# A hybrid attention and pooling block: pooling's splits and maps between the steps of the last k and q tiles, first loads issued there

## The chip, the cores and the metric

The kernel runs on one core of one Trainium2 chip. The metric is the device time of one execution in microseconds (us). Each core has five engines with queues of their own: TensorE (PE in the profile, its weight loads PEld), VectorE (DVE), ScalarE (ACT), GpSimd (POOL, here Pool) and SyncE (SP), which in this kernel only issues DMA transfers. Each engine works its queue strictly in order and waits on semaphores that the other engines and the transfers raise. Matmuls write into eight PSUM banks of 128 x 512 float32; a bank is used again when its reader has let it go.

## What is computed

One layer of a streaming encoder over 16 meta tokens and 1024 frames, 1024 wide. Cut to what matters here:

```python
n1 = _rmsnorm(h, norm1_w)
q, k, v, fg, u = jnp.split(n1 @ w_in, ...)
q, k = per-head rmsnorm of q and k
a_out = _forgetting_attention(q, k, v, cumsum(log_sigmoid(fg + b)))
pooled[g] = trailing mean of u[g] over 2, 4, 8, 16 frames - u[g]
p_out = einsum("blgc,gcd->blgd", pooled, w_pool) * pool_scale
h = h + concat(a_out, p_out) @ w_out
h = h + (silu(n2 @ w_gate) * (n2 @ w_up)) @ w_down
```

Every matrix product is done in three matmuls, on a high and a low part of each operand (high x high, high x low, low x high). So each operand is *split* first: ScalarE copies it into the high part (`A.activation(..., AF.Copy)`), and VectorE or Pool subtracts that from the original to give the low part.

## The kernel before

All tiles are transposed: features on the partitions, 1040 positions along the free axis. The program is one list in which the order for every engine is written by hand; closures that are put off go to the list `later`, and each call of `run_later` lets the next step of every pending tile run.

The input projection goes tile by tile in `order`: q0, k1, q1, k2, q2, then the four pooling groups u3 to u0, then k3 and q3. A k tile has three column chunks (348, 346, 346), a q tile two of 512, and each chunk takes 24 matmuls (`proj_mm`, tile `pj`, L446 to L448). `qk_evac` (from L306) does the head norm of a chunk in steps: ScalarE squares the bank twice (`sqh`, `sq`) and VectorE subtracts (`sql`, L312); one turn of `later` on, two matmuls sum over the head (`ss`, L316 and L317), VectorE adds, ScalarE takes logarithm and exponential, Pool multiplies (L322); a turn later VectorE does three more and so frees the bank (L325 to L327); then ScalarE's high part (L330), then VectorE's low part (L333) and, behind a tile's last chunk, the store of both parts to DRAM (L336).

Pooling: Pool adds shifted copies of u (L459), VectorE finishes (L464). In the last q tile, which runs its two chunks in step over eight k blocks of the input (L485 to L487), the four groups are split (L490, in the helper at L132), then the pool weights (L495); behind the tile `pool_map` maps each group with 2 x 3 matmuls (tile `pm`, L526 to L528), ScalarE and VectorE evict and split the result (`mph` L529, `mpl` L530).

Output projection: a job is one of eight row blocks and one half of the frames, 12 matmuls of 512 columns for the pooled half of the mix (tile `o`, L544 to L546). Its weights come by `out_load` (tile `wos`, L558), are split by ScalarE (L573) and Pool (L574), and VectorE adds the bank to a row of h, loaded by `h_load` (L565, add L603). The jobs wait in `fill_q`; `fill(1)` puts one into the program, and they serve as work for TensorE between the steps of attention.

Attention: `stack(h)` loads a head's q and k (L632 to L634), `vload(h)` its values (L639). A unit (h, b) is a head and one half of the frames. For each unit `mx_steps` computes scores (tile `s`, L666 to L669) whose maxima VectorE takes (`mp`, L670), and `mt` transposes the negated maxima (L689), after which the unit's steps run: logits (`st`), two exponentials on ScalarE, the low part `pl` on Pool or VectorE (L735), products with v (`pv`). Before the first unit come its scores and some output jobs; `RAMP` says how many times a job and two scores of the second unit are put ahead of the loop, and `FILL[n]` how much of a job goes into each step of unit n.

SP's queue takes its transfers in program order; a store that waits for its data holds those behind it.

Of the kernel before, what the change touches and what calls it, by code (L numbers as in the profile page):

```python
# [7 lines left out]
FT = mybir.dt.float32  # L8
FR = mybir.dt.float32r
AF = mybir.ActivationFunctionType  # L10
OP = mybir.AluOpType
# [3 lines left out]
KT = D // 128  # L15
META = 16
SEQ = 1024
L = META + SEQ
# [5 lines left out]
ST = 9  # L24
# [15 lines left out]
MID = 1  # L40
VST = 3
AGE = 2
RAMP = 2
FILL = [12 / 40] * 8 + [16 / 40] * 8


@with_exitstack
def block_kernel(ctx, tc, hT, n1w, w_f, w_v, w_u, w_qk, b_f, qnw, knw, w_pool, pscale, w_out, n2w, w_g, w_up, w_d, outT):
# [12 lines left out]
    def ut(cols, dt=FT, s="u"):  # L61
        return U.tile([128, cols], dt, tag="u", bufs=NU, padded_shape=None, name=nm(s))
# [4 lines left out]
    def ps(s="ps"):  # L67
        return PSP.tile([128, 512], FT, tag="ps", name=nm(s))
# [57 lines left out]
    def split_w(stage, cols, mk, he, le):  # L126
        h, l = mk(cols, FR, "wh"), mk(cols, FR, "wl")
        if he is A:
            A.activation(h, stage, AF.Copy)
        else:  # L130
            he.tensor_copy(h, stage)
        le.tensor_tensor(l, stage, f(h), op=OP.subtract)  # L132
        return h, l
# [6 lines left out]
    def aux(cols, dt=FT, s="ax"):  # L140
        return U.tile([128, cols], dt, tag="aux", bufs=NAUX, name=nm(s))
# [117 lines left out]
    def v_evac(j, p):  # L259
        sz = min(128, L - 128 * j)  # L260
        for i in range(2):
            if len(vst) < 2 * VST:
                t = ut(768, FR, "vst").rearrange("p (h c) -> p h c", c=192)
                V.tensor_copy(t[:, :, 64:128], onesf[:, None, 0:64].to_broadcast([128, 4, 64]))
                vst.append(t)
            t, src = vst[2 * (j % VST) + i], p[:sz, 256 * i:256 * i + 256].rearrange("p (h c) -> p h c", c=64)
            A.activation(t[:sz, :, 0:64], src, AF.Copy, scale=rcol[:sz, j:j + 1])
            V.scalar_tensor_tensor(t[:sz, :, 128:192], src, rcol[:sz, j:j + 1], f(t)[:sz, :, 0:64], op0=OP.mult, op1=OP.subtract)
            nc.sync.dma_start(vsd[j, :sz, 768 * i:768 * i + 768], f(t)[:sz].rearrange("p h c -> p (h c)"))
# [32 lines left out]
    def qk_tile(c, i):  # L302
        n = L if c == "k" else SEQ
        return c, i, n, ut(n, FT, c + "32"), ut(n, FR, c + "h"), ut(n, FR, c + "l")

    def qk_evac(p, n, cols, w, tile, C):  # L306
        name, i, width, t32, th, tl = tile
        out = t32[:, C]
        h, l, s = hs(n, FR, "sqh"), hs(n, FR, "sql"), hs(n, FT, "sq")
        A.activation(h, p[:, :n], AF.Square)  # L310
        A.activation(s, p[:, :n], AF.Square)
        V.tensor_tensor(l, s, f(h), op=OP.subtract)  # L312

        def rest():
            p2 = ps("ss")
            mm(p2[:, :n], bones, h, start=True, stop=False)  # L316
            mm(p2[:, :n], bones, l, start=False, stop=True)  # L317
            t, g, s2 = hs(n, FT, "t"), hs(n, FT, "g"), hs(n, FT, "s2")
            V.scalar_tensor_tensor(t, qrow[:, cols], 64.0 * EPS, p2[:, :n], op0=OP.mult, op1=OP.add)
            A.activation(g, t, AF.Ln)  # L320
            A.activation(g, g, AF.Exp, scale=-0.5)  # L321
            G.tensor_tensor(s2, t, g, op=OP.mult)  # L322

            def last():
                V.scalar_tensor_tensor(s2, s2, -0.5, g, op0=OP.mult, op1=OP.mult)  # L325
# [12 lines left out]
                later.append(high)  # L338
            later.append(last)
        later.append(rest)  # L340

    def run_later(now):
        for g in now:
            g()
# [8 lines left out]
    vp = vn  # L353
# [61 lines left out]
    def load_w(x):  # L415
        c, i = order[x]
        return load((w_u[i] if c == "u" else w_qk[2 * i + (c == "k")]).rearrange("p k f -> p (k f)"), 1024, aux)
# [23 lines left out]
    def proj_mm(w, o, n):  # L441
        wh, wl = w
        p = ps("pj")
        for k in range(KT):
            W = slice(128 * k, 128 * k + 128)
            mm(p[:, :n], wh[:, W], xh[k][:, o:o + n], start=k == 0, stop=False)  # L446
            mm(p[:, :n], wl[:, W], xh[k][:, o:o + n], start=False, stop=False)  # L447
            mm(p[:, :n], wh[:, W], xl[k][:, o:o + n], start=False, stop=k == KT - 1)  # L448
        return p
# [14 lines left out]
            V.scalar_tensor_tensor(pooled[g], src[:, META:], 1.0 / (2 << g), pooled[g], op0=OP.mult, op1=OP.subtract)  # L464
        late_u.append(last)

    v_evac(ST - 1, vp)
    for x, (c, i) in enumerate(order):
        if x + 2 < len(order):
            staged.append(load_w(x + 2))  # L470
        if c == "u":
            t = ut(L, FT, "u")
        else:
            t = qk_tile(c, i)
        if x + 1 == len(order):

            now, later[:] = later[:], []
            run_later(now)
            wps = aux(512, FT, "wps")
            nc.sync.dma_start(wps, w_pool.rearrange("p g f -> p (g f)"))  # L480
            pb = [ps("pj") for _ in CHQ]
            for k in range(KT):
                W = slice(128 * k, 128 * k + 128)
                for p, (o, n) in zip(pb, CHQ):
                    mm(p[:, :n], wcur[0][:, W], xh[k][:, o:o + n], start=k == 0, stop=False)  # L485
                    mm(p[:, :n], wcur[1][:, W], xh[k][:, o:o + n], start=False, stop=False)
                    mm(p[:, :n], wcur[0][:, W], xl[k][:, o:o + n], start=False, stop=k == KT - 1)  # L487
                if k % 2:
                    g = 3 - k // 2
                    psplit[g] = split_w(pooled[g], SEQ, ut, A, V)  # L490
                if k == 2:
                    now, later[:] = later[:], []
                    run_later(now)
                if k == 4:
                    wph, wpl = split_w(wps, 512, aux, A, V)  # L495
            for p, (o, n) in zip(pb, CHQ):
                qk_evac(p, n, slice(o, o + n), qw, t, slice(o - META, o - META + n))
            break
        for o, n in CHQ if c == "q" else CH3:
            p = proj_mm(wcur, o, n)  # L500
            if o < 512 and n + o < 600 and x + 1 < len(order):
                wnext = split_w(staged.pop(0), 1024, ut, A, V)
            now, later[:] = later[:], []
            if o > 512 and late_u:
                late_u.pop(0)()
            if c == "u":
                V.tensor_tensor(t[:, o:o + n], p[:, :n], rb[:, o:o + n], op=OP.mult)
            else:
                a = o - META if c == "q" else o
                qk_evac(p, n, slice(o, o + n), kw if c == "k" else qw, t, slice(a, a + n))  # L510
            run_later(now)
        if c == "u":
            pool(i, t)
        wcur = wnext


    mixp = [None] * 4

# [95 lines left out]

    vhb = [[ut(192 * nj, FR, "vh").rearrange("p (j c) -> p j c", c=192) for nj in (5, 4)] for _ in range(2)]
    Mc = [const([128, 4, 68], FR, f"Mc{i}") for i in range(2)]
    for t in Mc:
        G.memset(f(t), 0.0)  # L620
# [13 lines left out]
        dma(f(K2)[64:68], f(KAT[0])[4 * h:4 * h + 4])  # L634

    def vload(h):
        for t, j, n, sz in ((0, 0, 5, 128), (1, 5, 3, 128), (1, 8, 1, 16)):
            o = j - 5 * t
            nc.sync.dma_start(f(vhb[h % 2][t])[:sz, o:o + n], vsd[j:j + n, :sz, 192 * h:192 * h + 192].rearrange("j p c -> p j c"))  # L639
# [148 lines left out]

    units = [(h, b) for h in range(NH) for b in range(2)]
    out_fill(0, lambda: mixp, ((4, 8),), range(0, 8), True)  # L790
    wo0 = out_load(0)
    out_fill(4, lambda: mixa[0:2], ((0, 2),), range(0, 8), False)
    wo[0] = out_split(wo0)
    h_load(0)
    wo[1] = out_load(1)
    stack(0)
    vload(0)
    for g in (3, 2, 1, 0):
        pool_map(g)
        now, later[:] = later[:], []  # L800
        run_later(now)
    s0 = mx_steps(*units[0])
    for x, s in enumerate(s0):
        s()
        if x % 2:
            fill(1)
            now, later[:] = later[:], []
            run_later(now)
    while later:
        now, later[:] = later[:], []  # L810
        run_later(now)
    stack(1)
    fin = mt(*units[0])
    fill(1)
    fin()
# [635 lines left out]
```

## Time and profile before

| | us |
|---|---|
| median of 3 runs | 1159.59 (1158.83 to 1160.97) |
| the profiled execution | 1161.34 |
| its span, first to last instruction | 1159.6 |
| TensorE busy | 1127.5 |
| VectorE, ScalarE, Pool busy | 747.6, 478.1, 373.9 |
| mean granted TensorE clock | 0.938 of full speed |

The span is what the profile's times are counted in, from its first instruction. Busy time says what an engine worked, not what it held up; for that there are the list of waits, the timeline of each engine and the windows, which give busy time and granted clock for a stretch. The last k tile begins at about 197 us, attention at about 254, the second half of the layer at about 488.

### The profile page before, as it was taken

The numbers are of one execution on the slowest core, as the hardware profiler recorded it, in microseconds if no ns is written. First come the engines' busy times: TensorE is split into PE (matmuls) and PEld (weight loads), VectorE is DVE, ScalarE is ACT, GpSimd is POOL, SyncE is SP. The second block draws the span as 40 slices with busy tenths as digits, with TensorE's granted clock in tenths as the row PEclk, the third lists the DMA queues.
The fourth block names the chain that finished last, engine by engine and source line by source line (L and its number), as shares of the span: only waits on it lengthen the run. The fifth ranks groups of instructions, "written<-read, shape, count | busy, mean of one in ns | idle before, by whom it ended". The sixth has DMA issues, their size and how long they took to land.

```text
span 1159.6 us, 14738 instructions
## 1 busy us (share of the span) xinstructions
PE 1127.5 (97%) x5327; PEld 932.9 (80%) x5327; DVE 747.6 (64%) x1185; ACT 478.1 (41%) x868; POOL 373.9 (32%) x292
## 2 busy tenths in 40 slices
PE   7999999889999999888999999999999999999998
PEld 6778899778888888666788888888888888888886
DVE  7555873764556676799654554455545569778976
ACT  7344531624555666534332332233123335343532
POOL 0001244223434556538644345334533510000000
PEclk9889999988999999899899999999999999999999
DMA  7133340574544343230323132213221379543452
GB/s 240 75 131 144 125 145 33 138 220 101 138 107 99 93 98 114 100 118 0 109 73 95 52 109 73 96 50 110 73 82 64 132 256 373 187 158 100 153 193 109
DMA packets 62425, 141.10 MB, mean 122 GB/s; under 512 B 7616, under 2 KB 18496, under 8 KB 62352
## 3 DMA queue, kind: packets, MB, share of 16 engines
q1 hardware_dynamic: 52528, 123.86, 33.6%
q10 hardware_dynamic: 9824, 16.30, 3.8%
q8 instruction: 42, 0.69, 0.2%
q14 instruction: 31, 0.25, 0.1%
HBM read 105.17 MB, written 34.77 MB: 121 GB/s over the span
## 4 chain that ended last, share of the span: by engine, by line
PE 83%; DVE 8%; DMA 3%; ACT 2%; issue 2%; POOL 1%; SPq 0%; ACTq 0%; POOLq 0%; DVEq 0%
PE gu L1118 10%; PE gu L1117 10%; PE gu L1116 10%; PE d L1358 6%; PE d L1360 6%; PE d L1359 6%; PE pj L447 3%; PE pj L448 3%; PE pj L446 3%; PE o L544 2%; PE st L721 2%; PE o L545 2%; PE o L546 2%; PE v L254 2%; PE v L255 2%
## 5 line engine op out<-in xcount | busy, mean ns | idle before, releaser
L1117 PE MATMUL gu<-cb,ws 128*128 128x512 f32 x560 | 221.1, 395 | 4.2 <-DVE ws L1107 4.1
L1118 PE MATMUL gu<-cb,ws 128*128 128x512 f32 x560 | 221.0, 395 | 0.0
L1116 PE MATMUL gu<-cb,ws 128*128 128x512 f32 x560 | 221.0, 395 | 0.0
L1107 DVE TENSOR_TENSOR ws<-wst,ws 128x512 fp32r<-128x512 f32 x120 | 97.1, 809 | 124.9 <-ACT ws L1106 124.9
L1117 PEld LDWEIGHTS gu<-cb,ws 128*128 128x128 f32 x560 | 105.6, 189 | 29.8 <-DVE ws L1107 5.1
L1106 ACT ACTIVATE ws<-wst 128x512 fp32r<-128x512 f32 x120 | 69.9, 621 | 137.4 <-POOL wst L1101 129.7
L1118 PEld LDWEIGHTS gu<-cb,ws 128*128 128x128 f32 x560 | 105.7, 189 | 24.6
L1116 PEld LDWEIGHTS gu<-cb,ws 128*128 128x128 f32 x560 | 105.4, 188 | 24.3
L1358 PE MATMUL d<-hd,wd 128*128 128x512 f32 x308 | 121.4, 394 | 0.0
L1359 PE MATMUL d<-hd,wd 128*128 128x512 f32 x308 | 121.2, 394 | 0.0
L1360 PE MATMUL d<-hd,wd 128*128 128x512 f32 x308 | 121.2, 394 | 0.0
L735 POOL TENSOR_TENSOR pl<-p,ph 128x512 fp32r<-128x512 f32 (+4 forms) x66 | 72.6, 1112 | 56.9 <-ACT p L729 47.9
L1130 POOL TENSOR_TENSOR e<-e,e 128x512 f32<-128x512 f32 x20 | 29.6, 1479 | 158.2 <-DVE e L1143 105.4
L447 PE MATMUL pj<-xh,wl 128*128 128x346 f32 (+2 forms) x216 | 72.9, 337 | 0.0
L448 PE MATMUL pj<-xl,wh 128*128 128x346 f32 (+2 forms) x216 | 72.8, 337 | 0.0
L446 PE MATMUL pj<-xh,wh 128*128 128x346 f32 (+2 forms) x216 | 72.8, 337 | 0.0
L322 POOL TENSOR_TENSOR s<-t,g 128x346 f32<-128x346 f32 (+2 forms) x20 | 22.2, 1118 | 155.3 <-ACT g L321 144.6
L670 DVE TENSOR_REDUCE mp<-s 128x1 f32<-128x144 f32 (+6 forms) x112 | 52.5, 504 | 30.3 <-PE s L669 28.4
L728 ACT ACTIVATE ph<-st 128x512 fp32r<-128x512 f32 (+4 forms) x88 | 46.4, 528 | 58.4 <-PE st L721 55.2
L1360 PEld LDWEIGHTS d<-hd,wd 128*128 128x128 f32 x308 | 57.9, 188 | 13.5
L1359 PEld LDWEIGHTS d<-hd,wd 128*128 128x128 f32 x308 | 57.9, 188 | 13.3
L1358 PEld LDWEIGHTS d<-hd,wd 128*128 128x128 f32 x308 | 57.9, 188 | 13.4
(287 smaller groups left out, 2525.2 us busy)
## 6 DMA issues: line engine op xcount, KB each, us to landing
wst<-in_w_d SPq DMA_DIRECT2D x77, 256.0 KB, 3.4
wst<-in_w_g SPq DMA_DIRECT2D x22, 512.0 KB
wst<-in_w_up SPq DMA_DIRECT2D x22, 512.0 KB, 3.4
wst<-hidd SPq DMA_DIRECT2D x22, 512.0 KB, 7.7
K<-kd SPq DMA_DIRECT2D x24, 260.0 KB, 6.6
vsd<-vst SPq DMA_DIRECT2D x16, 384.0 KB, 2.4
Q<-qd SPq DMA_DIRECT2D x24, 256.0 KB, 7.8
wst<-in_w_d SPq DMA_DIRECT2D x11, 512.0 KB, 5.8
```

The lines of the kernel that those rows point to most:

```text
L446: mm(p[:, :n], wh[:, W], xh[k][:, o:o + n], start=k == 0, stop=False)
L447: mm(p[:, :n], wl[:, W], xh[k][:, o:o + n], start=False, stop=False)
L448: mm(p[:, :n], wh[:, W], xl[k][:, o:o + n], start=False, stop=k == KT - 1)
L735: sub.tensor_tensor(pl[:sz, o0:o1], p32[:sz, o0:o1], f(ph)[:sz, o0:o1], op=OP.subtract)
L1106: A.activation(t[:, :512], src, AF.Copy)
L1107: E.tensor_tensor(t[:, 512:], src, f(t)[:, :512], op=OP.subtract)
L1116: mm(p, w[:, W], c[:, :512], start=k == 0, stop=False)
L1117: mm(p, w[:, Wl], c[:, :512], start=False, stop=False)
L1118: mm(p, w[:, W], c[:, 512:], start=False, stop=k == 3)
L1358: mm(p, w[:, W], h[:, LO], start=i == 0, stop=False)
L1359: mm(p, w[:, Wl], h[:, LO], start=False, stop=False)
L1360: mm(p, w[:, W], h[:, HI], start=False, stop=i == NPR - 1)
```

## The change

It moves code; no instruction is added or left out on TensorE. Four parts:

- The pooled groups 3, 2 and 1 are split after the three chunks of the last k tile, the pool weights after the third; group 0 after the first of the eight steps of the last q tile. The four maps stand between its steps 2 to 6. The ss pair of k's third chunk stands behind the first step.
- `out_load` of the first two jobs, `h_load` of the first two rows and head 0's `stack` and `vload` are issued in the last k tile and the first two steps of q; the first weights are split after step 6.
- Behind the q tile, each of five output jobs is followed by a turn of `later` and (from the second on) one score step; `stack(1)` stands in the third of these.
- `RAMP` is 1, and `FILL` 11/37 for the first eight units, 17/40 for the others.

```diff
-RAMP = 2
-FILL = [12 / 40] * 8 + [16 / 40] * 8
+RAMP = 1
+FILL = [11 / 37] * 8 + [17 / 40] * 8
...
             run_later(now)
+            if x + 2 == len(order):
+                psplit[3 - a] = split_w(pooled[3 - a], SEQ, ut, A, V)
+                if a == 2:
+                    wo[0] = out_load(0)
+                    wph, wpl = split_w(wps, 512, aux, A, V)
...
+    for k in range(KT):
...
+        turn()
+        if k == 0:
+            psplit[0] = split_w(pooled[0], SEQ, ut, A, V)
+            h_load(0)
+            wo[1] = out_load(1)
+        if k == 1:
+            h_load(1)
+            stack(0)
+            vload(0)
+        if 2 <= k < 6:
+            pool_map(5 - k)
+        if k == 6:
+            wo[0] = out_split(wo[0])
...
-    for x, s in enumerate(s0):
-        s()
-        if x % 2:
-            fill(1)
-            now, later[:] = later[:], []
-            run_later(now)
-    while later:
-        now, later[:] = later[:], []
-        run_later(now)
-    stack(1)
+    for x in range(5):
+        fill(1)
+        turn()
+        if x:
+            s0.pop(0)()
+        if x == 2:
+            stack(1)
+    s0.pop(0)()
     fin = mt(*units[0])
     fill(1)
     fin()
```

Three places in the queues. First TensorE where the last k tile ends (`ss` of its third chunk, `pj` the banks of the q tile), before and now:

```order
L316 MATMUL ss_1940<-sqh_1918,bones 128x346
L317 MATMUL ss_1940<-sql_1919,bones 128x346
L485 MATMUL pj_1956<-xh_127,wh_1841 128x512
L486 MATMUL pj_1956<-xh_127,wl_1842 128x512
L487 MATMUL pj_1956<-xl_128,wh_1841 128x512
L485 MATMUL pj_1957<-xh_127,wh_1841 128x512
```

```order
L786 MATMUL pj_1966<-xh_127,wh_1849 128x512
L787 MATMUL pj_1966<-xh_127,wl_1850 128x512
L788 MATMUL pj_1966<-xl_128,wh_1849 128x512
L786 MATMUL pj_1967<-xh_127,wh_1849 128x512
L787 MATMUL pj_1967<-xh_127,wl_1850 128x512
L788 MATMUL pj_1967<-xl_128,wh_1849 128x512
L316 MATMUL ss_1974<-sqh_1934,bones 128x346
L317 MATMUL ss_1974<-sql_1935,bones 128x346
L786 MATMUL pj_1966<-xh_156,wh_1849 128x512
```

The pair ss went behind six matmuls of the q tile.

Second SP's queue behind the loads for head 0 (`kd`, `qd` the stores of the last tiles, `wos` output weights, `h` rows of h, `Q`, `K` head 1), before and now, each as far as the first loads of head 1:

```order
L336 DMA kd<-kl_1815 128x1040
L336 DMA qd<-qh_1938 128x1024
L336 DMA qd<-ql_1939 128x1024
L558 DMA wos_2182<-in_w_out 128x512
L565 DMA h_374_2184<-in_hT 128x1024
L632 DMA Q_381_2230<-qd 64x1024
L632 DMA K_383_2232<-kd 64x1040
```

```order
L336 DMA kd<-kh_1822 128x1040
L336 DMA kd<-kl_1823 128x1040
L509 DMA wos_2140<-in_w_out 128x512
L509 DMA wos_2204<-in_w_out 128x512
L516 DMA h_376_2206<-in_hT 128x1024
L583 DMA Q_380_2231<-qd 64x1024
L583 DMA K_382_2233<-kd 64x1040
```

The two stores of q went behind; now they stand after all eight transfers of `stack(1)`:

```order
L585 DMA K_383_2234<-kat_702 4x1040
L336 DMA qd<-qh_1964 128x1024
L336 DMA qd<-ql_1965 128x1024
L509 DMA wos_2267<-in_w_out 128x512
L516 DMA h_387_2269<-in_hT 128x1024
L509 DMA wos_2329<-in_w_out 128x512
L516 DMA h_396_2331<-in_hT 128x1024
```

Third VectorE ahead of the second unit's mt (`h` the adds of output jobs, `mp` the maxima of scores, `mx` and `Mc` the three small steps that mt waits for), before and now:

```order
L670 TENSOR_REDUCE mp_2295<-s_2327 128x1
L670 TENSOR_REDUCE mp_2295<-s_2331 128x1
L603 TENSOR_TENSOR h_387_2249<-o_2311,h_387_2249 128x512
L670 TENSOR_REDUCE mp_2295<-s_2367 128x1
L670 TENSOR_REDUCE mp_2295<-s_2371 128x1
L670 TENSOR_REDUCE mp_2295<-s_2402 128x1
L670 TENSOR_REDUCE mp_2295<-s_2406 128x1
L670 TENSOR_REDUCE mp_2295<-s_2410 128x1
L682 TENSOR_REDUCE mx_2415<-mp_2295 128x4
L683 TENSOR_SCALAR Mc_2048<-mx_2415 128x4
L684 SCALAR_TENSOR_TENSOR Mc_2048<-mx_2415,Mc_2048 128x4
```

```order
L554 TENSOR_TENSOR h_387_2269<-o_2333,h_387_2269 128x512
L623 TENSOR_REDUCE mp_2349<-s_2391 128x1
L623 TENSOR_REDUCE mp_2349<-s_2395 128x1
L623 TENSOR_REDUCE mp_2349<-s_2426 128x1
L623 TENSOR_REDUCE mp_2349<-s_2430 128x1
L623 TENSOR_REDUCE mp_2349<-s_2435 128x1
L623 TENSOR_REDUCE mp_2349<-s_2439 128x1
L623 TENSOR_REDUCE mp_2349<-s_2443 128x1
L635 TENSOR_REDUCE mx_2448<-mp_2349 128x4
L636 TENSOR_SCALAR Mc_830<-mx_2448 128x4
L637 SCALAR_TENSOR_TENSOR Mc_830<-mx_2448,Mc_830 128x4
```

The add in the middle moved two maxima up, and the row it adds to is that of the fourth job, not of the third. In the programs for TensorE, five score steps now stand between the second unit's logits ahead and its mt, where there were three; unit (3, 1) has no output job in place of two, and seven stand ahead of the loop in place of five.

## Rows read from the trace of the kernel before

**Rows 1.** the page's busy times: engine, us, share of the span, instructions.

```profile
PE 1127.5 (97%) x5327; PEld 932.9 (80%) x5327; DVE 747.6 (64%) x1185; ACT 478.1 (41%) x868; POOL 373.9 (32%) x292
```

**Rows 2.** who waited for whom, TensorE, 205 to 268.7: us in total, times, longest.

```profile
PE mt L689 <- DVE Mc L684: 2.6, 1, 2.6
PE s L666 <- DVE mpl L530: 2.2, 1, 2.2
PE o L544 <- DVE q L327: 2.0, 1, 2.0
PE ss L317 <- DVE sql L312: 0.5, 1, 0.5
```

**Rows 3.** windows: length, busy PE, PEld, DVE, ACT, POOL; clock, DMA share, GB/s.

```profile
231.15:240.26 9.11, 7.01 (x21) 5.52 (x22) 8.97 (x13) 3.83 (x7) 1.28 (x1) 0.61 0.29 116
...
261.25:268.66 7.41, 7.27 (x22) 5.42 (x22) 0.49 (x1) 1.67 (x3) 1.29 (x1) 0.57 0.00 0
360.00:380.00 20.00, 19.55 (x126) 17.06 (x124) 11.96 (x24) 12.99 (x27) 9.66 (x9) 0.95 0.37 84
```

**Rows 4.** timeline of TensorE: start, us, line, operation, out<-in [idle before <-releaser].

```profile
208.53 0.32 PE L317 MATMUL ss<-sql,bones 128*128 128x346 f32 x1
...
210.26 0.40 PE L485 MATMUL pj<-xh,wh 128*128 128x512 f32 x1
...
235.00 0.63 PE L545 MATMUL o<-mph,wo 128*128 128x512 f32 x1
235.43 0.63 PE L546 MATMUL o<-mpl,wo 128*128 128x512 f32 x1
...
243.86 0.40 PE L544 MATMUL o<-mph,wo 128*128 128x512 f32 x1
...
246.64 0.41 PE L689 MATMUL mt<-ident,Mc 128*68 128x128 f32 x4
...
261.25 0.64 PE L689 MATMUL mt<-ident,Mc 128*68 128x128 f32 x4 [2.65 <-DVE Mc L684]
```

**Rows 5.** groups by form, 195 to 300: xcount | busy us, mean ns | idle before.

```profile
L574 POOL TENSOR_TENSOR wo<-wos,wo 128x512 fp32r<-128x512 f32 x6 | 7.7, 1289 | 35.8 <-ACT wo L573 27.3 <-DMA Q<-qd 8.5
...
L530 DVE SCALAR_TENSOR_TENSOR mpl<-pm,psc,mph 128x512 fp32r<-128x512 f32 x8 | 5.6, 743 | 2.5 <-ACT mph L529 2.5
...
L529 ACT ACTIVATE mph<-pm,psc 128x512 fp32r<-128x512 f32 x8 | 4.9, 688 | 0.0
L132 DVE TENSOR_TENSOR wl<-u,wh 128x1024 fp32r<-128x1024 f32 x4 | 4.8, 1224 | 0.6 <-ACT wh L129 0.6
...
L129 ACT ACTIVATE wh<-u 128x1024 fp32r<-128x1024 f32 x4 | 4.1, 1043 | 0.0
...
L322 POOL TENSOR_TENSOR s<-t,g 128x346 f32<-128x346 f32 x2 | 1.9, 944 | 4.3 <-ACT g L321 4.3
...
L312 DVE TENSOR_TENSOR sql<-sq,sqh 128x346 fp32r<-128x346 f32 x2 | 1.0, 520 | 5.3 <-ACT sq L311 5.3
...
L132 DVE TENSOR_TENSOR wl<-wps,wh 128x512 fp32r<-128x512 f32 x1 | 0.7, 691 | 0.0
```

**Rows 6.** timeline of VectorE ahead of the second unit's mt.

```profile
257.54 0.69 DVE L603 TENSOR_TENSOR h<-o,h 128x512 f32<-128x512 f32 x1 [2.74 <-DMA h<-in_hT]
258.15 2.44 DVE L670 TENSOR_REDUCE mp<-s 128x1 f32<-128x456 f32 x5
```

**Rows 7.** timeline of SP's queue, the store of ql and the h load.

```profile
241.26 0.32 SPq L336 DMA_DIRECT2D qd<-ql  x1
...
250.80 0.33 SPq L565 DMA_DIRECT2D h<-in_hT  x1
```

**Rows 8.** timeline of Pool: an add of pooling, and the pl at attention's end.

```profile
164.43 2.29 POOL L459 TENSOR_TENSOR uw<-u 128x1039 f32<-128x1039 f32 x1 [3.85 <-DVE u L507]
...
460.80 1.30 POOL L735 TENSOR_TENSOR pl<-p,ph 128x512 fp32r<-128x512 f32 x1
```

**Rows 9.** timeline of VectorE, a weight split beside Pool's add.

```profile
165.15 2.66 DVE L132 TENSOR_TENSOR wl<-wst,wh 128x1024 fp32r<-128x1024 f32 x1 [0.20 <-ACT wh L129]
```

More of the change, by code (lines that the diff above doesn't have):

```diff
@@ L465, in pool @@
         late_u.append(last)
[L467 to L475, printed above, removed]
-            now, later[:] = later[:], []
-            run_later(now)
[L479 to L491, printed above, removed]
-                    now, later[:] = later[:], []
-                    run_later(now)
[L494 to L514, printed above, removed]
     mixp = [None] * 4
@@ L613, in out_fill @@
             fill_q.extend([(need, lambda x=x: out_job(x, 0)), (need, lambda x=x: out_job(x, 1))])
-    vhb = [[ut(192 * nj, FR, "vh").rearrange("p (j c) -> p j c", c=192) for nj in (5, 4)] for _ in range(2)]
+    vhb = []
     Mc = [const([128, 4, 68], FR, f"Mc{i}") for i in range(2)]
@@ L636, in vload @@
     def vload(h):
+        if h < 2:
+            vhb.append([ut(192 * nj, FR, "vh").rearrange("p (j c) -> p j c", c=192) for nj in (5, 4)])
         for t, j, n, sz in ((0, 0, 5, 128), (1, 5, 3, 128), (1, 8, 1, 16)):
@@ L790, in block_kernel, with turn @@
     out_fill(0, lambda: mixp, ((4, 8),), range(0, 8), True)
-    wo0 = out_load(0)
     out_fill(4, lambda: mixa[0:2], ((0, 2),), range(0, 8), False)
[L793 to L799, printed above, removed]
+    def turn():
         now, later[:] = later[:], []
         run_later(now)
-    s0 = mx_steps(*units[0])
-    for x, s in enumerate(s0):
-        s()
-        if x % 2:
-            fill(1)
-            now, later[:] = later[:], []
-            run_later(now)
@@ L809, in block_kernel @@
-    while later:
-        now, later[:] = later[:], []
-        run_later(now)
-    stack(1)
+    v_evac(ST - 1, vp)
+    for x, (c, i) in enumerate(order[:-1]):
+        if x + 2 < len(order):
+            staged.append(load_w(x + 2))
+        else:
+            wps = aux(512, FT, "wps")
+            nc.sync.dma_start(wps, w_pool.rearrange("p g f -> p (g f)"))
+        t = ut(L, FT, "u") if c == "u" else qk_tile(c, i)
+        for a, (o, n) in enumerate(CHQ if c == "q" else CH3):
+            p = proj_mm(wcur, o, n)
+            if o < 512 and n + o < 600:
+                wnext = split_w(staged.pop(0), 1024, ut, A, V)
+            now, later[:] = later[:], []
+            if o > 512 and late_u:
+                late_u.pop(0)()
+            if c == "u":
+                V.tensor_tensor(t[:, o:o + n], p[:, :n], rb[:, o:o + n], op=OP.mult)
+            else:
+                S = slice(o - META, o - META + n) if c == "q" else slice(o, o + n)
+                qk_evac(p, n, slice(o, o + n), kw if c == "k" else qw, t, S)
+            run_later(now)
+            if x + 2 == len(order):
[3 more added lines that the diff above has]
+                    wph, wpl = split_w(wps, 512, aux, A, V)
+        if c == "u":
+            pool(i, t)
+        wcur = wnext
@@ new lines, in block_kernel @@
+    t = qk_tile(*order[-1])
+    pb = [ps("pj") for _ in CHQ]
+    for k in range(KT):
+        W = slice(128 * k, 128 * k + 128)
+        for p, (o, n) in zip(pb, CHQ):
+            mm(p[:, :n], wcur[0][:, W], xh[k][:, o:o + n], start=k == 0, stop=False)
+            mm(p[:, :n], wcur[1][:, W], xh[k][:, o:o + n], start=False, stop=False)
+            mm(p[:, :n], wcur[0][:, W], xl[k][:, o:o + n], start=False, stop=k == KT - 1)
+        turn()
[11 more added lines that the diff above has]
+            wo[0] = out_split(wo[0])
@@ L813, in block_kernel @@
+    for p, (o, n) in zip(pb, CHQ):
+        qk_evac(p, n, slice(o, o + n), qw, t, slice(o - META, o - META + n))
+    s0 = mx_steps(*units[0])
+    for x in range(5):
[6 more added lines that the diff above has]
+    s0.pop(0)()
     fin = mt(*units[0])
```

## Prediction

> **What bounds the kernel now.** I read the page first: TensorE's matmuls are busy for 97% of the span [rows 1], so time can only come from stretches where it waits or runs slowly. Next the list of who waited for whom, cut to 205 to 268.7 us, the stretch that the change rewrites: four waits that matter, 2.6, 2.2, 2.0 and 0.5 us, 7.3 together [rows 2]. Then the windows of that stretch: in 231.15 to 240.26 and 261.25 to 268.66 the mean granted clock is 0.61 and 0.57, between 1.2 and 2.4 GHz, while a window in attention has 0.95 [rows 3]. Both falls follow the long waits, and the price of a fall shows in the pitch: two matmuls of 512 columns stand 0.43 us apart at the low level; at the high one twelve take 2.78 us, 0.23 each [rows 4]. So the stretch loses twice, by waiting and then by the slow clock. The other engines only matter here for what they release late.
>
> How much it loses, I take from the work between two points. From the end of the last k tile's second ss pair (208.53 and one more matmul, 208.70) to the transposes of the second unit (mt, 261.25) [rows 4] there are 52.6 us. The same instructions at the high clock: 48 matmuls of the last q tile at 0.231, 11.1 us; 24 of the maps and four ss of 512 columns at the same, with two ss of 346, 6.8; five output jobs of 2.78, 13.9; the score and logit products and the first mt, about 14,200 columns, 6.4 at 0.231 per 512, and 7.5 as I take it, since the small ones run slower than their columns. That is 39.3, so 13.3 are lost. Behind 261.25, seven output matmuls and three pv at 0.43 instead of 0.23 cost 2.0, and mt, st and what is left 1.0. **Lost in all: 16.3 us.**
>
> **The change part by part.** Both orders have the same number of TensorE rows, so no work goes; it is put where TensorE waited.
>
> - *The ss pair of the last k chunk* now has six q matmuls ahead of it, 6 x 0.23 = 1.4 us. Before, it cost 208.70 to 210.26 less its own 0.3, 1.2 us. But VectorE now has a split (1.22) and the last step of pooled group 0 (as wide, 1.2) ahead of that chunk's sql (0.52) [rows 5], where it had only the latter behind it. Adding up its queue from 208.25, where ScalarE, after chunk 1's squares and exponentials and 1.04 for the high part [rows 5], hands that over, gives sql at 211.0; TensorE stands there from 210.2. A new wait of 0.8.
> - *The first map* needs the split of the pool weights, now emitted between k and q. VectorE's queue behind 211.0: three steps of chunk 0 as wide as its sql (1.65), a wait for ScalarE's 1.04, a split of 1.22 and the one of half its width (0.69) [rows 5]: 215.3, TensorE is there at about 214.4. A wait of 0.9. The other maps stand 1.4 us of q matmuls apart, while ScalarE and VectorE need 2 x 0.69 and 2 x 0.74 for one map [rows 5], nearly the same pace, and they have the two last q steps to catch up; I charge nothing. If that cover went, the fourth map would wait for the first one's banks, about a us.
> - *The first output job* comes straight after q, at 227.4. Its weights' low part is ScalarE behind eight map evictions, then Pool for 1.29 [rows 5]: 228.1. A wait of 0.7.
> - *The waits of 2.2 and 2.0 us* [rows 2] were for banks that VectorE freed late, behind a chain of q's norm steps. Those steps now run under seven output jobs (19.5 us) with one score step between two, instead of all scores and two jobs. By my sum the q banks are free at 239.5, and TensorE wants the first of them at 241.6: these two waits and the first fall of the clock go.
> - *SP's queue.* Before, the h row for the third job stood behind the store of ql, issued at 241.26, and behind stack(1); it was issued at 250.80, and VectorE sat 2.74 us in front of its add until 257.54, with five reduces behind it (2.44) and mt behind those [rows 6, 7]. Now that row, the third and fourth jobs' weights and stack(1) are ahead of both q stores. What SP is moved past are the two waits for q's high and low part; who waits for these stores is only stack of a later head. The next h row (job 4) goes out at about 244.5 and at the 6.7 us from 250.80 to 257.5 lands near 251.2, just when the add comes; reduces behind it have some 3 us to spare.
> - *The second unit's mt.* RAMP = 1 leaves five scores in one go ahead of it instead of three. VectorE takes 2.44 for five and 0.6 for the three small steps behind [rows 6]: with a start at 255.3 the mt can run at 258.2 and TensorE is there at 256.2. A wait of 2.0, in place of 2.6.
> - *Mc's fills and two small casts* move from the crowded VectorE of the last q tile to the first one; nobody in TensorE's list of waits asks for them [rows 2]. Nothing charged; at most two instructions the size of a map's 0.74 [rows 5] either way.
> - *Early loads* (stack(0), h, weights) move by some us in a queue that no TensorE wait names; nothing.
> - *FILL and RAMP* take two output jobs, 5.6 us, out of unit (3, 1), where they were cover, to the front. In 360 to 380, which has none either, TensorE still works 19.55 of 20 us [rows 3]; so I charge 0.5 (bounds 0 and 3, half a us for each of six steps). One job of the later set leaves the drain at the end of attention, so that two pv stand in a row; the second needs Pool's pl of 460.80, 1.30 long [rows 8], which I charge at 0.6 (bounds 0 and 1.3).
>
> **Sum.** New waits 0.8 + 0.9 + 0.7 + 2.0 = 4.4, with start-ups 4.7 (bounds 2, the last wait alone, and 9, each twice as long); lost cover 1.1 (0 and 4.3). 16.3 - 4.7 - 1.1 = **10.5 us less**. The profiled execution took 1161.34, so 1150.8; the median shown, 1159.59, lies 1.75 below it, so 1149.1, and I write 1149.3.
>
> **Two engines on one memory.** The splits are the terms that could swell: one of 1024 columns took 2.66 us at 165.15, while Pool's add ran from 164.43 [rows 8, 9], against 1.22 for those at 214 to 221 [rows 5]. In the new place Pool runs three products of about 0.9 us [rows 5] in the time of the splits. They hang on each other (Pool waits for ScalarE's exponentials, and ScalarE's part of the next split goes after those), so I count none; if each met one, VectorE's chain would be 3 x 0.9 = 2.8 us later, and the gain 7.7.
>
> The Trainium skill ("SBUF — State Buffer", Who interferes with whom) says that a VectorE instruction with two SBUF inputs and a GpSimd instruction that reads SBUF lock each other out, one of them for the whole of the other. The long split agrees with that. Were it met at every split, it would be the first rival.
>
> **The rivals.** (1) *The splits meet Pool's products*: 2.8 us on VectorE's chain, and the pool weights, the maps and the q banks come that much later: 10.5 - 2.8 = 7.7, 1151.9. For it the split of 2.66 [rows 9], against it the order in which they hang on each other. (2) *Part comes back with the clock*: the wait of 2.0 at mt, or two in the q tile that run into each other, reach the 2.2 from which the clock fell, and it falls once more. Six us at 0.43 instead of 0.23 cost 2.8, with up to 3 more of waits: gain 4.5 to 7.7, 1151.9 to 1155.1. For it: by my sum VectorE is nearly full from 204 to 246. Against it: no single new wait is over 2.0, and the 0.5 at the ss pair left the clock as it was [rows 2]. (3) *No change*: VectorE's chain slips by 5 us, q's banks come late again and the two waits with their fall return, 2.2 + 2.0 + 2.8 = 7.0: gain 3.5, and with one more fall 0.7, 1156.1 to 1158.9. The slack of 2 us at the banks speaks against it. (4) *Slower*: unit (3, 1) and the steps after it, up to the first later job in (4, 1), have no output job between them. If each of these 14 steps waits for Pool's pl (1.3, [rows 8]) behind two exponentials, 0.8 a step is 11, and two falls of the clock add 5.6: 17 lost against the 11 won in front, 1165. It decides from about 0.55 us a step on. The 0.45 us that TensorE is short of in all of 360 to 380 [rows 3] speaks strongly against it. (5) *More than forecast*: VectorE keeps up and none of the small waits shows, gain 12 to 14.6, 1145.0 to 1147.6.
>
> **How the numbers follow.** Forecast (gain 8 to 12) 0.54; (1) 0.12; (2) 0.14; (3) 0.06; (4) 0.04; (5) 0.10. The range goes from the end of (5) past (2) to the near end of (3), 1145 to 1156; what of (3) and (4) lies outside, and what I have not thought of, is about 0.15. About 0.2%, 2.3 us, is what a measurement of this kernel can tell from no change. Below 1157.3 lie the forecast, (1), (2), (5) and the nearer part of (3): faster 0.89. The farther part of (3) and half of what I have not thought of: the same 0.06. (4): slower 0.05.
>
> **What would show it.** Right: in the new trace no TensorE wait over 2.2 us and no low clock between the last k tile and the second unit's first logits; the ss pair waits on sql, the first map on the pool weights, the first output job on Pool; mt of the second unit is the longest; its time about 258, with two output jobs more behind it; no wait for h. Wrong: waits for a bank in the q tile or at the first scores; a clock of 1.2 GHz in that stretch; TensorE short of more than 2 us in unit (3, 1) and head 4; or the order of SP holding up a score.

## The result, and the profile after

The changed kernel takes 1152.95 us in the median of 4 runs (1152.78 to 1153.57), the kernel before 1160.28 on the same chip (1158.83 to 1161.35): ratio 0.9939, 95% interval 0.9921 to 0.9956. Run once more, beside experiments 5 to 7, it gave 1153.48 against 1159.63, ratio 0.9943 (0.9930 to 0.9956). It is faster, by 7.3 us where 10.5 were forecast. The profiled execution took 1152.78, its span is 1151.1.

The page's busy times, as in [rows 1]:

```profile
PE 1123.0 (98%) x5327; PEld 931.0 (81%) x5327; DVE 745.4 (65%) x1185; ACT 477.8 (42%) x868; POOL 374.4 (33%) x292
```

Who TensorE waited for, 205 to 268.7, the list of [rows 2]:

```profile
PE mt L642 <- DVE Mc L637: 1.5, 1, 1.5
PE pm L478 <- DVE wl L132: 0.8, 1, 0.8
PE ss L317 <- DVE sql L312: 0.7, 1, 0.7
PE st L674 <- ACT Q L643: 0.4, 1, 0.4
```

The waits of 2.2 for `mpl` and 2.0 for the q bank are gone, and the one for `Mc` is shorter. Windows (length, busy PE, PEld, DVE, ACT, POOL; clock, DMA share, GB/s): two that answer to [rows 3], and one that was not expected.

```profile
231.15:240.26 9.11, 9.11 (x45) 7.59 (x44) 7.32 (x9) 3.57 (x6) 4.25 (x3) 1.00 0.97 242
256.00:264.00 8.00, 6.35 (x33) 5.16 (x34) 3.08 (x10) 2.76 (x5) 1.29 (x1) 1.00 0.00 0
437.17:444.00 6.83, 6.22 (x15) 4.83 (x16) 2.78 (x4) 4.51 (x9) 4.86 (x5) 0.50 0.73 268
```

In the front TensorE keeps the high clock throughout. But at 437 there is a slow stretch that the kernel before did not have: its window there has 0.95 over 448 to 452, the same place of the program, and 0.95 is how that profile shows the undisturbed clock (last section).

```profile
448.00:452.00 4.00, 3.79 (x17) 2.69 (x17) 1.53 (x3) 3.84 (x8) 2.86 (x4) 0.95 0.60 157
```

The timeline of TensorE at that place, changed kernel (start, us, line, operation [idle before <-releaser]):

```profile
436.01 0.49 PE L671 MATMUL st<-Q,K 128*128 128x512 f32 x1
437.78 0.79 PE L674 MATMUL st<-Q,K 68*128 68x512 f32 x1 [1.27 <-ACT Q L643]
...
439.65 0.63 PE L495 MATMUL o<-mh,wo 128*128 128x512 f32 x1
440.08 0.63 PE L496 MATMUL o<-mh,wo 128*128 128x512 f32 x1
```

The first logits of head 7's second unit wait 1.27 us for ScalarE's copy of the transposed maxima into Q, and behind that the matmuls stand 0.43 us apart, as in [rows 4]. ScalarE's own timeline shows what stands ahead of the copy:

```profile
431.85 1.35 ACT L824 ACTIVATE wc<-wos 128x512 fp32r<-128x512 f32 x2 [0.77 <-DMA wos<-in_w_out]
433.82 0.63 ACT L824 ACTIVATE wc<-wos 128x512 fp32r<-128x512 f32 x1 [0.62 <-DMA wos<-in_w_out]
434.36 0.40 ACT L524 ACTIVATE wo<-wos 128x256 fp32r<-128x256 f32 x1
434.66 0.48 ACT L681 ACTIVATE ph<-st 128x400 fp32r<-128x400 f32 x1
435.05 0.49 ACT L682 ACTIVATE p<-st 128x400 f32<-128x400 f32 x1
436.48 0.63 ACT L824 ACTIVATE wc<-wos 128x512 fp32r<-128x512 f32 x1 [0.94 <-DMA wos<-in_w_out]
437.14 0.59 ACT L643 ACTIVATE Q<-mt 4x512 fp32r<-4x512 f32 x1
```

The transposes ran at 433.59. In front of the copy ScalarE has four `wc` copies, the weights of the last output jobs (`wc_prep`, from L820), with three waits for their loads, 2.3 us. The kernel before has the same block of work, but with an output job right ahead of the logits (six matmuls, 446.81 to 448.29, 1.5 us; the jobs of this part are half as long as those in front). The first and the last row of that place, kernel before:

```profile
446.81 0.50 PE L544 MATMUL o<-mh,wo 128*128 128x512 f32 x1
...
448.90 0.50 PE L721 MATMUL st<-Q,K 68*128 68x512 f32 x1 [0.21 <-ACT Q L690]
```

Its wait was 0.21 us, although its copy of Q starts 3.85 us behind the transposes (444.41 to 448.26) and that of the changed kernel 3.55 (433.59 to 437.14). So the copy is no later than it was; what is gone is the cover. The new `FILL` had put that job two steps earlier.

Two landmarks split the gain. The matmuls before the transposes of the ninth unit (head 4, first half) are the same set in both kernels, and so are those between it and the norm's first matmul (`n`). Kernel before, then the changed one:

```profile
362.37 0.40 PE L689 MATMUL mt<-ident,Mc 128*68 128x128 f32 x4
486.88 0.80 PE L857 MATMUL n<-wh,ones 128*128 128x512 f32 x1 [3.88 <-ACT wh L129]
```

```profile
350.31 0.42 PE L642 MATMUL mt<-ident,Mc 128*68 128x128 f32 x4
478.24 0.79 PE L857 MATMUL n<-wh,ones 128*128 128x512 f32 x1 [4.04 <-ACT wh L129]
```

At the first landmark the change is 12.06 us ahead, at the second 8.64, at the end of the span 8.5. So 3.4 us of what the front won are given back between head 4 and the norm: 127.9 us from mark to mark instead of 124.5. Half of the 6.83 us at half rate is just 3.4. In experiment 10 the same wait (1.26 us) stands without a slow stretch, and its profile has 124.5 us from mark to mark: the wait itself adds little.

### The profile page after: what moved, and what is told of

Read it like the earlier page. It is cut to its first block, busy times and chain, and to the rows that moved or that the text cites. A ratio compares the mean times of both kernels' runs of the same rounds, so it can differ in the third digit from the quotient of the medians.

```text
span 1151.1 us, 14746 instructions
## 1 busy us (share of the span) xinstructions
PE 1123.0 (98%) x5327; PEld 931.0 (81%) x5327; DVE 745.4 (65%) x1185; ACT 477.8 (42%) x868; POOL 374.4 (33%) x292
## 4 chain that ended last, share of the span: by engine, by line
PE 90%; DVE 6%; ACT 1%; issue 1%; DMA 1%; POOL 0%; SPq 0%; ACTq 0%; POOLq 0%; DVEq 0%
PE gu L1118 11%; PE gu L1117 11%; PE gu L1116 11%; PE d L1360 6%; PE d L1358 6%; PE d L1359 6%; PE pj L447 3%; PE pj L448 3%; PE pj L446 3%; PE o L495 2%; PE o L496 2%; PE o L497 2%; PE st L674 2%; PE pv L701 2%; PE s L622 2%; PE st L671 2%
## 5 line engine op out<-in xcount | busy, mean ns | idle before, releaser
L1107 DVE TENSOR_TENSOR ws<-wst,ws 128x512 fp32r<-128x512 f32 x120 | 97.2, 810 | 124.9 <-ACT ws L1106 124.9
```

The lines of the kernel that those rows point to most:

```text
L1107: E.tensor_tensor(t[:, 512:], src, f(t)[:, :512], op=OP.subtract)
```

## The experiments

Line numbers in rows of a variant are its own: those of the changed kernel, some lines further where a diff adds them, and in 3 those of the kernel before. Each ratio is to the kernel before on the same chip. **Theory A**: the front's rewrite wins 11 to 12 us, and one output job, moved by the new shares, uncovers the late copy of Q and so gives back about 4. The rivals are that the clock falls there anyway (B), or that the loss comes from head 3's missing jobs or from the start (C).

**1. That job back in its old place.**

```diff
             share += FILL[n]
+            share += {(14, 0): -1, (14, 2): 1}.get((n, x), 0)
```

> The changed kernel with one output job moved by two steps: from behind the first step of head 7's first unit to behind its third, where it stands right ahead of the next unit's first score tile. Theory A (the new position of that job uncovers the late copy of Q on ACT: 1.27 us of wait for it at 437.8 and 2.8 us of matmuls at the lower clock behind it): the wait falls under 0.3 us, no low clock in 430 to 446, 1148.9 us (1148.3 to 1149.6). Rival B (the clock falls there by the small matmuls ahead, whatever the wait): low clock still there, 1151.7 to 1152.5. Rival C (the missing time went elsewhere, to the jobs missing in head 3 or to the start): 1152.9, no change.

1151.27 us (1149.83 to 1152.27), ratio 0.9916 (0.9903 to 0.9930). The wait is gone and the clock stays up at 436 to 444, but a slow stretch stands at another place: behind the wait for `Mc`, which the first profile had without one. Windows of this kernel, and the transposes ahead of the first:

```profile
257.20:260.60 3.40, 3.31 (x8) 2.53 (x9) 0.00 (x0) 1.12 (x3) 1.26 (x1) 0.52 0.00 0
436.00:444.00 8.00, 7.71 (x38) 5.95 (x37) 4.73 (x7) 7.79 (x15) 6.44 (x6) 1.00 0.68 232
```

```profile
256.17 0.44 PE L642 MATMUL mt<-ident,Mc 128*68 128x128 f32 x4 [1.54 <-DVE Mc L637]
```

From mark to mark it needs 124.4 us (350.78 to 475.19), as the kernel before. So theory A holds for the place; rivals B and C fall. The median is 2.4 above A's number, and the slow stretch at 257 (half of 3.4 us is 1.7) explains it only in part.

**2. The old shares altogether.**

```diff
-FILL = [11 / 37] * 8 + [17 / 40] * 8
+FILL = [12 / 40] * 8 + [16 / 40] * 8
```

> The changed kernel with the old table of shares (12/40 and 16/40), everything else as changed. Head 3's second unit still has no output jobs; the second eight heads' jobs stand where they stood before. Theory A: 1148.9 us (1148.3 to 1150), no low clock in 430 to 450, no wait over 0.5 us for the copy of Q of head 7's second unit. Rival C (the loss is the missing cover in head 3, or lies in the start): 1152.9, no change.

1150.35 us (1150.07 to 1152.67), ratio 0.9914 (0.9900 to 0.9927); no wait for that copy, 124.9 us from mark to mark. Head 3 still lacks its two jobs here, so rival C falls again. A's range is missed by little: three of the four runs lie within 0.6 us of A's upper bound of 1150; the profiled one, 1152.67, again has a slow stretch at 260.

**3. The same job moved in the kernel before.**

```diff
             share += FILL[n]
+            share += {(14, 0): 1, (14, 2): -1}.get((n, x), 0)
```

> The kernel before with the one output job of head 7's first unit moved the other way, from behind the third step to behind the first; nothing else. Theory A: the score tile at 448.9 waits 1.3 us or more for the copy of Q (0.21 before) and the clock falls behind it: 1164.4 us (1163 to 1165.5). Rival B (wait without a fall): 1161.5. Rival C: 1160.3, no change.

1161.90 us (1160.09 to 1162.81), ratio 1.0009 (1.0000 to 1.0018). The mechanism came as A said, wait and fall:

```profile
448.66 0.50 PE L721 MATMUL st<-Q,K 68*128 68x512 f32 x1 [1.25 <-ACT Q L690]
```

```profile
449.70:453.10 3.40, 3.40 (x11) 2.75 (x10) 2.14 (x4) 3.20 (x6) 2.69 (x3) 0.55 0.92 348
```

Its price was overrated: the slow stretch is half as long as in the changed kernel, mark to mark takes 126.5 us, 2.0 more than before, and the median rose by 1.1. A's 1164.4 is missed; 1.1 us is what the runs give.

**4. The loads of those weights ahead of the copies.**

```diff
-            bg.extend([lambda i=i: wc_prep(i) for i in range(4)])
+            ld, pr = ([lambda i=i, g=g: g(i) for i in range(4)] for g in (wc_load, wc_prep))
+            bg.extend([ld[0], ld[1], ld[2], pr[0], ld[3], pr[1], pr[2], pr[3]])
```

> The changed kernel, its jobs where the change put them, but the four loads of the last weights issued a step ahead of the copies that wait for them (three at head 7's first step, the fourth with the first copies a step later). Theory A in its full form (the copy of Q is late because ACT stood 2.3 us waiting for these loads ahead of it): the waits of ACT for them fall under 0.5 us in sum, the score tile's wait for Q under 0.4, no low clock in 430 to 446, 1148.9 us (1148.3 to 1149.9). Rival A' (the copy is late whatever the loads do, by ACT's own work, and only a job in between covers it): wait 0.8 to 1.3 us and low clock as in the changed kernel, 1152 to 1153. Rival C: 1152.9.

1153.38 us (1152.46 to 1155.76), ratio 0.9937 (0.9925 to 0.9949): no gain. In the profile ScalarE no longer waits for loads, the copy of Q is in time, and no slow stretch follows. Instead the copies come in pairs, Pool subtracts in pairs, and the `pl` behind them is late:

```profile
440.58 2.52 POOL L830 TENSOR_TENSOR wc<-wos,wc 128x512 fp32r<-128x512 f32 x2 [0.63 <-ACT wc L829]
443.05 2.80 POOL L688 TENSOR_TENSOR pl<-p,ph 128x432 fp32r<-128x432 f32 x2
```

```profile
444.21 0.39 PE L703 MATMUL pv<-pl,vh 128*128 128x272 f32 x1 [2.14 <-POOL pl L688]
```

The edit moves two things at once: with the loads issued apart, only two of the four `wc` copies stand ahead of the copy of Q. So it shows that these copies and their loads hold Q up, but not that the loads alone do, and this cure trades one wait for another: 125.8 us from mark to mark.

**The changed kernel again**, as the measure for 5 to 7:

> The changed kernel itself once more, as the measure for the other kernels of this call on the same chip: 1152.9 us (1152 to 1154). What its profile is to tell: a stretch at the lower clock behind the 1.3 us wait for Q at 437 and none behind the 1.5 us wait for Mc at 257, as in the first profile (the two waits differ in kind), or one behind either of them (the same wait is followed by a slow stretch in some executions and by none in others; the three variants of the changed kernel that ran so far all had one at 257).

1153.48 us (1150.74 to 1153.66), ratio 0.9943. The slow stretch at 437 came again, none at 257.

**5. The four maps together behind the q tile.**

```diff
-        if 2 <= k < 6:
-            pool_map(5 - k)
...
+    for g in (3, 2, 1, 0):
+        pool_map(g)
     s0 = mx_steps(*units[0])
```

> The changed kernel with the four maps put together behind the q tile, where they stood before; the splits on DVE and ACT, the Pool-side work and all loads stay where the change put them. Theory A (the maps' evacuations, 8 times 0.69 on ACT and 0.74 on DVE, are hidden only between the q tile's steps): the wait of the maps' reads for wl in the q tile (0.8) goes, a wait for the q banks and for mpl of 2 to 3.5 us comes back behind the q tile with a slow stretch behind it in most executions: 1155 to 1158. Rival D (the early splits and loads are what the change gains, the maps' place is free): 1151.5 to 1153.

1152.71 us (1151.76 to 1153.75), ratio 0.9941 (0.9927 to 0.9954), the same as the changed kernel; rival D. The 0.8 us for `wl` goes and no wait for a bank comes; the head of the list from 196 to 470:

```profile
PE mt L642 <- DVE Mc L637: 2.2, 2, 1.5
PE st L674 <- ACT Q L643: 1.2, 1, 1.2
```

Putting the maps between the steps of q gains nothing.

**6. Both waits covered by an output job**: the first experiment's line, and

```diff
             if any(u == (h, b) for u, _, _ in fins):
+                if n == 1:
+                    fill(1)
                 finish(0)
```

> The kernel of the first experiment (the output job back ahead of head 7's second unit) with one output job more put ahead of the transposes of head 0's second unit, where the changed kernel waits 1.54 us for Mc. Theory A: neither the wait for Mc at 257 nor the wait for Q at 437, no slow stretch between 75 and 470: 1147.5 us (1146.5 to 1148.5). Rival E (the wait only moves, to the next unit or to the place in head 3 that loses its last job): 1150 to 1151.5, a new PE wait of over 1 us between 258 and 360.

1148.42 us (1147.23 to 1148.70), ratio 0.9900 (0.9885 to 0.9915); again beside the ninth: 1149.09, 0.9901 (0.9886 to 0.9916). It is 5.1 us less than the changed kernel run beside it. Both windows keep the high clock:

```profile
255.00:265.00 10.00, 9.61 (x50) 7.80 (x50) 4.73 (x13) 3.05 (x6) 2.64 (x3) 1.00 0.92 211
433.00:443.00 10.00, 9.56 (x45) 7.38 (x45) 5.84 (x8) 9.61 (x20) 7.75 (x8) 1.00 0.62 224
```

**7. The first loads behind the q tile.**

```diff
-            h_load(0)
-            wo[1] = out_load(1)
-        if k == 1:
-            h_load(1)
-            stack(0)
-            vload(0)
...
+    h_load(0)
+    wo[1] = out_load(1)
+    h_load(1)
+    stack(0)
+    vload(0)
     s0 = mx_steps(*units[0])
```

> The changed kernel with only the first loads of attention and of the output projection (the two residual rows, the second job's weights, head 0's Q, K and V) issued behind the q tile's last step instead of between its first steps. Theory A (the early issue hides some 9 us of issue and landing): the first score of head 0, due two output jobs behind the q tile, waits 2 to 5 us for K and Q, with a slow stretch behind it in most executions: 1156 to 1160. Rival D' (the loads were hidden anyway by the jobs that now come first): 1152 to 1154.

1158.02 us (1156.11 to 1161.23), ratio 0.9989 (0.9979 to 0.9999): of a gain of 0.6% a tenth of a per cent is left. The first score waits for head 0's K, twice:

```profile
235.09 0.46 PE L619 MATMUL s<-K,Q 128*128 128x144 f32 x1 [2.47 <-DMA K<-kd]
238.16 0.46 PE L622 MATMUL s<-K,Q 66*128 66x144 f32 x1 [2.42 <-DMA K<-kd]
```

These are 4.9 us of waiting, a slow stretch of 6.8 us starts at 234.7, and the median rose by 4.5.

**8. Splits and maps where they stood before**, loads early:

```diff
-                psplit[3 - a] = split_w(pooled[3 - a], SEQ, ut, A, V)
...
-                    wph, wpl = split_w(wps, 512, aux, A, V)
...
+        if k % 2:
+            psplit[3 - k // 2] = split_w(pooled[3 - k // 2], SEQ, ut, A, V)
+        if k == 4:
+            wph, wpl = split_w(wps, 512, aux, A, V)
```

and the maps as in the fifth.

> The changed kernel with the splits of the four pooled rows and of the pool weights back inside the q tile (behind its second, fourth, sixth and eighth step, the weights' behind its fifth) and, as this makes necessary, the maps behind the q tile, whose place by itself made no difference in the fifth experiment. The early loads and the steps of the evacuations between the q tile's steps stay. Theory A (in the q tile the splits stand ahead of the q evacuations on DVE and Pool's work of the last k and q tiles): the waits for the q banks and for mpl of before come back, 2 to 4.5 us, with a slow stretch of 1.7 to 3.4 behind: 1156.5 to 1160. Rival F (of the three things that were moved only the loads count): 1152 to 1154 as the changed kernel.

1151.67 us (1150.66 to 1153.68), ratio 0.9928 (0.9915 to 0.9940): not slower than the changed kernel, rival F. In the list of waits from 196 to 470 a map's 1.0 for `mpl` stands in place of 0.8 for `wl` and 0.7 for `sql`:

```profile
PE mt L642 <- DVE Mc L637: 2.3, 2, 1.6
PE st L674 <- ACT Q L643: 1.3, 1, 1.3
PE pm L477 <- DVE mpl L481: 1.0, 1, 1.0
```

It is the fourth map that waits, by the "about a us" that the prediction named for it without its cover. So the part that names this change, the splits and maps between the steps, gains nothing that the runs show, the other parts being kept.

**9. The sixth kernel with the maps behind the q tile**, both edits as above.

> The sixth experiment's kernel (both waits covered by an output job) with the maps together behind the q tile. Theory A: only the wait of the maps for wl in the q tile (0.8 us) goes: 1147.6 us (1146.8 to 1148.6), against 1148.4 for the sixth kernel. Rival: the maps' evacuations put the first job or the transposes late now that no other wait hides them: 1149 or more, a wait for mpl or q of over 0.5 us between 225 and 262.

> The sixth experiment's kernel once more, beside the ninth on the same chip: 1148.4 us (1147.2 to 1149).

1146.55 us (1144.38 to 1147.02), ratio 0.9877 (0.9863 to 0.9890), against 1149.09 for the sixth on the same chip: the best of all, 14.0 us under the kernel before. It was to be 0.8 better and is 2.5. The spans of the profiles of both, taken beside each other, differ by 2.9 us: 1.1 of them lie ahead of the ninth unit, but 2.0 behind the norm's first matmul, in instructions that both have alike. There the slow stretch at 536 is 6.8 us long in the sixth and 3.4 in this one. So more than the 0.8 is not shown to come from the maps.

**10. The start of attention put back too**, on top of the eighth:

```diff
-    for x in range(5):
-        fill(1)
-        turn()
-        if x:
-            s0.pop(0)()
-        if x == 2:
-            stack(1)
-    s0.pop(0)()
+    for x, s in enumerate(s0):
+        s()
+        if x % 2:
+            fill(1)
+            turn()
+    while later:
+        turn()
+    stack(1)
```

with `RAMP = 2` and a turn behind each map.

> The kernel of the eighth experiment (splits and maps where they stood before, loads early) with the start of attention put back as well: the first score right behind the maps, output jobs behind the second and fourth score only, head 1's copies behind them, RAMP 2. What then remains of the change is the early issue of the first loads, the steps of the evacuations between the q tile's steps and the new table of shares. Theory A2 (the five output jobs that now stand ahead of and between the first scores cover the q tile's evacuations; without them a job waits about 2 us for the q banks or the transposes for Mc, with a slow stretch at 230 to 265): 1154.5 to 1158. Rival G (the early loads alone carry the gain of the front): 1151 to 1153, as the eighth kernel with 1151.7.

1156.23 us (1155.51 to 1158.76), ratio 0.9971 (0.9961 to 0.9982): 0.43% above the eighth, 5 us. A2 holds; the waits of [rows 2] are back, all of them (the list from 196 to 470):

```profile
PE mt L642 <- DVE Mc L637: 3.2, 2, 2.8
PE st L674 <- ACT Q L643: 1.6, 2, 1.3
PE o L495 <- DVE q L327: 1.6, 1, 1.6
PE ss L317 <- DVE sql L312: 1.4, 1, 1.4
PE s L619 <- DVE mpl L481: 1.1, 1, 1.1
```

```profile
230.20:233.60 3.40, 2.76 (x7) 2.21 (x8) 3.33 (x6) 1.40 (x3) 0.00 (x0) 0.52 0.00 0
257.50:260.90 3.40, 3.40 (x9) 2.54 (x10) 0.00 (x0) 1.09 (x2) 1.28 (x1) 0.52 0.00 0
```

VectorE's wait for the h row, 2.74 in [rows 6], is back as well:

```profile
252.57 0.69 DVE L554 TENSOR_TENSOR h<-o,h 128x512 f32<-128x512 f32 x1 [2.55 <-DMA h<-in_hT]
```

What this kernel still gains on the one before, 0.3%, is not in the list of waits, which is as long. Its two slow stretches are of 3.4 us, those in the windows of [rows 3] of 6.8. Whether the early loads or the turns between the q steps did that was not tried apart.

## Why the prediction was right, and where its sum failed

Direction and range were right, and so was most of the front. The time is not in the forecast's own band (gain 8 to 12, 1147.6 to 1151.6) but where rivals 1 and 2 lie; that the range held owes much to its width. From profiled execution to profiled execution the gain is 8.6 us, from median to median 7.3, since the kernel before was profiled in the slowest of its four runs. By the prediction's steps:

- *The front.* Forecast were 16.3 us lost before, 4.7 of them to come back as new waits, 0.5 of cover, so 11.1 gained at the ninth unit. Measured in the two profiles: 12.06. No stretch at 1.2 GHz is left there. That is in part luck: experiments 1 and 4 have the same instructions up to head 7, and a slow stretch of 3.4 us behind mt's wait.
- *The new waits*, place by place: the ss pair 0.8, measured 0.72; the first map 0.9, measured 0.84; the second unit's mt 2.0 at about 258, measured 1.54 at 257.26. The first output job's 0.7 shrank to one step of 0.38 instead of 0.23 behind its first matmul. The numbers given for the first map add up to 215.6, not 215.3, and so to a wait of 1.2; the pool weights' low part was ready at 214.6. The two of the q tile had the releasers that were named, as mt had:

```profile
210.35 0.43 PE L317 MATMUL ss<-sql,bones 128*128 128x346 f32 x1 [0.72 <-DVE sql L312]
214.64 0.50 PE L478 MATMUL pm<-wh,wl 128*128 128x512 f32 x1 [0.84 <-DVE wl L132]
```

- *SP's queue and the h row* went as laid out: the row is issued at 245.18, behind both stores of q, the add at 251.23 waits for no transfer, and five reduces in one go follow, as in [rows 6, 7]:

```profile
251.23 0.68 DVE L554 TENSOR_TENSOR h<-o,h 128x512 f32<-128x512 f32 x1
...
254.15 2.45 DVE L623 TENSOR_REDUCE mp<-s 128x1 f32<-128x456 f32 x5 [1.29 <-PE s L622]
```

- *"Those steps now run under seven output jobs"* was the right reason for the two big waits: taking the jobs away (10) brings them back and costs 5 us.
- *"Early loads: nothing."* This failed. With the maps gone from behind the q tile only two jobs are left to cover head 0's loads, and without their early issue K is 4.9 us late (7). The loads bring no gain of their own that the runs show, but most of the rest is lost without them. Late loads with the maps behind q, as in the kernel before, were not run, so that the maps were the cover is argued.
- *Rival 1, splits that meet Pool*, did not come: all four splits of the pooled rows take 1.22 or 1.23 us, and Pool's products (206.60, 211.91, 216.14, 0.94 each) overlap none of them by more than 0.1 us. But two engines did meet on the q tile's own steps, which the prediction had not looked at. Pool's two products there, and VectorE's step L325 beside the second of them and alone:

```profile
232.84 2.55 POOL L322 TENSOR_TENSOR s<-t,g 128x512 f32<-128x512 f32 x2 [2.43 <-ACT g L321]
234.18 1.77 DVE L325 SCALAR_TENSOR_TENSOR s<-s,g 128x512 f32<-128x512 f32 x1 [1.65 <-POOL s L322]
238.35 0.68 DVE L325 SCALAR_TENSOR_TENSOR s<-s,g 128x512 f32<-128x512 f32 x1
```

VectorE's next step takes 1.67 instead of 0.69 beside a weight split on Pool (235.34, 1.76 long). That is 2.1 us lost on VectorE; the last q bank came free at 240.5, where 239.5 was forecast, and TensorE did not wait. What the prediction cites from the Trainium skill ("SBUF — State Buffer", Who interferes with whom) agrees with these rows.
- *FILL and RAMP*, charged at 0.5 and 0.6. **This is the step that failed.** Neither place named cost anything: TensorE shows no wait in unit (3, 1), and the two pv of the drain run on without one. The cost was in a third place that the sum did not look at, head 7's second unit, where the moved job had covered ScalarE's late copy, and there it was the slow clock behind the wait: 3.4 us between the marks of the profiles, about 0.25%, 2.9 us, of the median (ratios of 0.9914 and 0.9916 in 1 and 2, 0.9939 and 0.9943 with the change). 12.06 less 3.4 is the 8.6 that the profile shows at the norm. The step had looked at units that lost a job, not at jobs that changed their step.
- *Rival 2's condition* failed too. It let the clock fall only from a wait of 2.2 on, since 0.5 had left it up. One more fall and a time within rival 2's span is what came, but behind 1.27 us and in head 7, while the rival had looked at the q tile and at mt.

The kernels with both waits covered (6 and 9) show the sum: 2.8 us of waits taken away, 5.1 us gained in 6.

## What to carry to other kernels

When a table of shares moves filling work, list for each step that loses a job what the engines behind it have in hand at that moment; a job two steps earlier is no cover, and units that keep their number of jobs can lose the one that mattered. Price a wait of TensorE like these (1.2 us and more) by the slow stretch that may follow it, and put one short job in front of it before anything else is moved. Of a change with several parts undo each by itself: here undoing the part in the foreground cost nothing, and undoing either of the two beside it, early loads and jobs between the first scores, about 5 us.

## What was not expected of the hardware

The same wait is not always followed by the low clock. Eight profiles have the wait of 1.54 or 1.55 us for `Mc` at the second unit; five of them have a slow stretch that starts at its end or up to 2.2 us behind it (experiments 1, 2, 4, 5, 8) and three none (the changed kernel twice, and 7). The wait of 1.2 to 1.3 us for Q has one in six of seven, starting from 0.6 us before its end on, of 6.8 us in both profiles of the changed kernel and of 3.4 in the other four; 10 has none, and neither has the wait of 2.14 in experiment 4. Where neither wait is left (6 twice, 9) no slow stretch stands between 75 and 460. The time goes by the stretch: from mark to mark the kernels that have the wait for Q need 124.5 us without one, 126.1 to 126.5 with 3.4 us of it (3, 5, 7, 8) and 127.9 with 6.8; the kernel before and those in which the job covers it (1, 2, 6, 9) need 123.9 to 124.9.

Which wait is followed by a slow stretch differs where the instructions up to it are the same, as at 257 in the changed kernel (none) and in 1 and 4 (3.4 us). Slow stretches also make part of the spread of one kernel's runs: the two profiles of the changed kernel differ by 2.1 us in span, 2.0 of it ahead of the ninth unit, where the first has two stretches of 3.4 us, at 48 and 65, and the second none. The Trainium skill ("TensorE: Matmul & The Clock Gate", What's actually happening) says that what sets the clock is "free-running — it doesn't reset when your kernel starts"; that agrees with these rows, where the same instructions after the same wait run at either level.

The mean granted clock of two profiles is no measure by itself: 0.938 before and 0.989 after, but the undisturbed level is shown as 0.95 in the one and 1.00 in the other, with twelve matmuls at 0.23 us each in both.
